# Chunk 5 of each up projection by seven block products instead of eight

## The chip, the cores and the metric

The program runs on one core of one Trainium2 chip. The metric is the device time of one execution in microseconds (us), the median of several runs. TensorE (PE) does the matrix products and loads their stationary operand in a queue of its own (PEld), VectorE (DVE) and ScalarE (ACT) do the elementwise work, GpSimd (POOL) very little, and SyncE (SP) issues the loads of the weights.

## The reference

The reference is a decoder trunk of two layers on 256 tokens of 1024 columns, in float32. Each layer is a half-weighted feed-forward, a token mixer, and a second half-weighted feed-forward; a final RMSNorm follows. So there are four feed-forwards, and the change concerns these alone:

```python
D_MODEL, SEQ, D_FF = 1024, 256, 2816
def swiglu(h, w_up, w_down):
    gate, up = jnp.split(h @ w_up, 2, axis=-1)     # w_up: 1024 x 5632
    return (jax.nn.silu(gate) * up) @ w_down       # w_down: 2816 x 1024
# four times:
x = x + 0.5 * swiglu(rmsnorm(x, norm), w_up, w_down)
```

## The kernel before

Every float32 operand is split in two, `hi` (a rounded copy) and `lo` (what is left), and each product of the reference is three matmuls (`mm3`, lines 302 to 304): hi by hi, hi by lo, lo by hi, added up in PSUM. The stationary operand is a 128 by 128 piece of the transposed activations (`xT_hi`, `xT_lo`), the moving one a piece of the weights.

The weights come in blocks of 128 by 1024 elements (512 KB), in the one order that the list `stream` gives. `feed` (line 180 on) makes a block ready: a load on SP's queue into a buffer `w`, a rounded copy into `hi` on ACT (line 200), and a subtraction into `lo` on DVE (line 201). `block` hands the next block to the matmuls and has fed four further ones by then (`LOOKAHEAD = 4`); there are five `hi` and five `lo` buffers, so the copy for a block waits until PE has finished the block five places ahead of it. The order of the instructions on each engine is laid down when the program is built: an operation whose inputs will be there may be put ahead of one that the code names earlier.

A feed-forward (`ffn`) computes `gate` and `up` in column chunks of 512 (`CW`). 2816 columns make five whole chunks, 0 to 4, and a chunk 5 with 256 columns of gate and 256 of up. Chunk 0 is done plainly. Chunks 1 and 3 are done by seven block products in Winograd's form of Strassen's scheme (`seven_and`, line 445 on): tokens, contraction and (gate, up) are each cut in two halves, and seven products P1 to P7 of half-sized blocks take the place of eight. In return the weights have to be added up in four ways (`form`, line 160 on, DVE adds at line 163; their operands lie in ten buffers `raw`), seven blocks have to be split instead of four for the same work, and the products have to be combined (DVE at line 416, results in buffers `post`). Their blocks alternate in `stream` with those of a plain chunk, 2 or 4, which forms the pair (1, 2) and the pair (3, 4).

Chunk 5 follows the pair (3, 4). It is done plainly: four blocks, each of two rows of 128 by 512 columns (256 of gate, 256 of up, loaded by two transfers of 256 KB), and for each row of 128, each of the two token halves and each of the three parts one matmul of 512 columns: 48 matmuls. Its outputs go through SiLU (ACT, line 420) and a product (DVE, line 425), and `turn` transposes them on PE (line 436) and splits them into `gT_hi` and `gT_lo` (lines 256, 257). `turn` starts two blocks after it was spawned, so the eight transposes of chunk 3 fall into chunk 5. Then the down projection (`y`) runs: two halves of 11 blocks, 12 matmuls of 512 columns each.

Of the kernel before, what the change touches and what calls it, by code (L numbers as in the profile page):

```python
# [15 lines left out]
ALU = mybir.AluOpType  # L16
# [3 lines left out]
P = 128  # L20
D = 1024
S = 256
NT = S // P
KD = D // P
FF = 2816
# [3 lines left out]
CW = 512  # L29
BLK = 1024  # L30
# [15 lines left out]
def trunk(ctx, tc, a, out):  # L46
    nc = tc.nc
# [11 lines left out]
    def pA(name):  # L59
        return psA.tile([P, CW], F32, tag="acc", name=name)  # L60

    def pB(name):
        return psB.tile([P, CW], F32, tag="mx", name=name)
# [7 lines left out]
    def cut(runs):  # L71
        r = []
        for k0, nk, n, cols in runs:
            kb = min(nk, BLK // n)
            for k in range(k0, k0 + nk, kb):
                kk = min(kb, k0 + nk - k)
                at, pieces = 0, []
                for w, c, m in cols:
                    pieces.append((at, m, w[k * P:(k + kk) * P, c:c + m].rearrange("(k p) c -> p k c", p=P)))
                    at += m  # L80
                r.append((kk, n, pieces))
        return r
# [3 lines left out]
    def one(w, k0, nk, c, n=CW):  # L86
        return (k0, nk, n, [(w, c, n)])

    def seven(w, c, mate):

        def cols(c):
            return (c * CW, FF + c * CW)

        def quarter(i, j, p):
            r0 = (4 * i + 2 * p) * P
            return w[r0:r0 + 2 * P, cols(c)[j]:cols(c)[j] + CW].rearrange("(k p) c -> p k c", p=P)

        gate, up = (cut([one(w, 0, 8, x)]) for x in cols(mate))
        st = {}
        r = []  # L100
        for x in SEVEN:
            if x[0] == "P":
                r += [(x, p, st, quarter) for p in range(2)]
            else:
                r.append((gate if x[0] == "G" else up)[int(x[1])])
        return r

    def up_runs(w, first=False):
        r, c = [], 0
        while c < 5:  # L110
            mate = dict(PAIRS).get(c)
            if mate is None:
                g, u = c * CW, FF + c * CW
                r += cut(([one(w, 0, 1, g), one(w, 1, 1, g), one(w, 2, 6, g)] if first and c == 0 else
                          [one(w, 0, 8, g)]) + [one(w, 0, 8, u)])
                c += 1
            else:
                r += seven(w, c, mate)
                c = mate + 1
        return r + cut([(0, 8, CW, [(w, 5 * CW, 256), (w, FF + 5 * CW, 256)])])  # L120

    def down_runs(w):
        return [one(w, 0, KF, 0), one(w, 0, KF, CW)]
# [23 lines left out]
    spool = [None]  # L147
    loaded = [0]

    def load(x, p, st, quarter):  # L150

        def raw(nm):
            if nm not in st:
                st[nm] = spool[0].tile([P, BLK], F32, tag="raw", name="raw", bufs=RAW_BUFS)
            return st[nm]

        for nm, i, j in {"P1": (("a", 0, 0),), "P6": (("b", 0, 1), ("d", 1, 1)), "P2": (("c", 1, 0),)}.get(x, ()):
            nc.sync.dma_start(out=raw(nm + str(p)).rearrange("p (k n) -> p k n", n=CW), in_=quarter(i, j, p))

    def form(x, p, st):  # L160

# [18 lines left out]
    def feed():  # L180
        i = pos[1]
        while loaded[0] < len(stream) and loaded[0] <= i + LEAD:
            if isinstance(stream[loaded[0]][0], str):
                if spool[0] is None:
                    break
                load(*stream[loaded[0]])
            loaded[0] += 1
        pos[1] += 1
        hi = wpool.tile([P, BLK], F32R, tag="hi", name=f"hi{i}", bufs=S_BUFS)
        lo = wpool.tile([P, BLK], F32R, tag="lo", name=f"lo{i}", bufs=S_BUFS)  # L190
        if isinstance(stream[i][0], str):
            k, n = 2, CW
            w = form(*stream[i][:3])
        else:
            k, n, pieces = stream[i]
            w = wpool.tile([P, BLK], F32, tag="w", name=f"w{i}", bufs=W_BUFS)
            wv = w[:, :k * n].rearrange("p (k n) -> p k n", n=n)
            for at, m, src in pieces:
                nc.sync.dma_start(out=wv[:, :, at:at + m], in_=src)
        nc.scalar.copy(out=hi[:, :k * n], in_=w[:, :k * n])  # L200
        nc.vector.tensor_tensor(out=lo[:, :k * n], in0=w[:, :k * n], in1=hi[:, :k * n].bitcast(F32), op=ALU.subtract)  # L201
        ready.append((k, hi[:, :k * n].rearrange("p (k n) -> p k n", n=n),
                      lo[:, :k * n].rearrange("p (k n) -> p k n", n=n)))
# [12 lines left out]
    def spawn(g, steps=1):  # L216
        tasks.append(g)
        speed[g] = steps
        return g
# [81 lines left out]
    def mm3(ps, xh, xl, wh, wl, start, stop, more=False):  # L301
        nc.tensor.matmul(ps, lhsT=xh, rhs=wh, start=start, stop=False, skip_group_check=more)  # L302
        nc.tensor.matmul(ps, lhsT=xh, rhs=wl, start=False, stop=False, skip_group_check=more)  # L303
        nc.tensor.matmul(ps, lhsT=xl, rhs=wh, start=False, stop=stop, skip_group_check=more)  # L304

    def xs_run(pss, hi, lo, k0, nk, kmin=0, kmax=KD - 1, t_major=False):

        k = k0
        while k < k0 + nk:
            kk, wh, wl = block()  # L310
            parts = [(k + i, wh[:, i, :], wl[:, i, :]) for i in range(kk)]
            k += kk
            if t_major and k + 4 > k0 + nk:
                while k < k0 + nk:
                    kk, wh, wl = block()
                    parts += [(k + i, wh[:, i, :], wl[:, i, :]) for i in range(kk)]
                    k += kk
            order = [(p, t) for p in parts for t in range(NT)]
            if t_major and k == k0 + nk:
                order.sort(key=lambda o: o[1])  # L320
            for (ki, whi, wli), t in order:
                mm3(pss[t], hi[:, ki, t * P:(t + 1) * P], lo[:, ki, t * P:(t + 1) * P], whi, wli,
                    ki == kmin, ki == kmax)
            tick()
# [45 lines left out]
    def ffn(n, nxt):  # L370
        with tc.tile_pool(name="gpool", bufs=1) as gpool:
# [30 lines left out]
            def product(x, ps, more=False):  # L402

                hi, lo = forms[x]
                for p in range(2):
                    kk, wh, wl = block()
                    for i in range(kk):
                        mm3(ps, hi[:, 2 * p + i, :], lo[:, 2 * p + i, :], wh[:, i, :], wl[:, i, :],
                            not more and p == 0 and i == 0, p == 1 and i == kk - 1, more)
                    tick()  # L410

            def post(nm):
                return gpool.tile([P, CW], F32, tag="post", name=nm, bufs=4)

            def tt(out, in0, in1, op=ALU.add):
                nc.vector.tensor_tensor(out=out, in0=in0, in1=in1, op=op)

            def silu(src, t, width=CW):
                s = work.tile([P, CW], F32, tag="og", name="s")
                nc.scalar.activation(out=s[:, :width], in_=src, func=AF.Silu, scale=n.rstd[:, t:t + 1])  # L420
                return s

            def times(src, s, t, width=CW):
                g = work.tile([P, CW], F32, tag="on", name="g")
                nc.vector.scalar_tensor_tensor(out=g[:, :width], in0=src, scalar=n.rstd[:, t:t + 1],
                                               in1=s[:, :width], op0=ALU.mult, op1=ALU.mult)
                return g
# [13 lines left out]
            def chunk_out(c, gate, up, width):  # L441
                gs = [times(up[t], silu(gate[t], t, width), t, width) for t in range(NT)]
                next(spawn(turn(c, gs, width)))

            def seven_and(c, mate):
# [28 lines left out]
                tt(q, pc, q, ALU.subtract)  # L474
                next(spawn(turn(c, [times(q, s0, 0), times(r, s1, 1)], CW)))

            spool[0] = gpool
            whole("P1", 0, 0)
            whole("P2", 1, 0)
            whole("P4", 1, 1)  # L480
            c = 0
            while c < 6:
                if c == 0:
                    sm = spawn(sums())
                if c in dict(PAIRS):
                    finish(sm)
                    seven_and(c, dict(PAIRS)[c])
                    c = dict(PAIRS)[c] + 1
                    continue
                gate = [pA("gate") for _ in range(NT)]  # L490
                up = [pB("up") for _ in range(NT)] if c < 5 else None
                xs_run(gate, xT_hi, xT_lo, 0, 8)
                if c < 5:
                    xs_run(up, xT_hi, xT_lo, 0, 8)
                    chunk_out(c, gate, up, CW)
                else:
                    chunk_out(c, [p[:, :256] for p in gate], [p[:, 256:] for p in gate], 256)
                c += 1
            for hf in range(2):
                y = [pA("y") for _ in range(NT)]  # L500
# [769 lines left out]
```

## Time and profile before

| | us |
|---|---|
| median of 3 runs | 1014.79 (1014.54 to 1015.05) |
| the profiled execution's own time | 1013.34 |
| its span, first to last instruction | 1011.6 |
| PE busy | 993.1 |
| DVE busy | 790.3 |
| ACT busy | 574.7 |
| the four stretches of chunk 5, each | 11.77 to 11.81 |

The profiled execution took 1013.34 us, 1.45 us less than the median of the runs. Times in the rows are microseconds from the start of the span. A matmul's duration in the profile runs past the start of the next one, since they are pipelined; the distance between two starts tells what one costs in a row of them. The same holds for DVE: the distance of two starts is what an operation in a row costs.

### The profile page before, as it was taken

What the parts mean: (1) busy time and instruction counts of PE and PEld (TensorE: products, weight loads), DVE (VectorE), ACT (ScalarE), POOL (GpSimd) and SP (SyncE); (2) the same over time, 40 slices, a digit from 0 to 9 for tenths busy, and PEclk for the clock granted to TensorE, in tenths of its full rate; (3) what the DMA queues carried; (4) which work ended last, traced back from release to release, by engine and by line L of the source; (5) the groups of instructions that cost most, each with busy time, mean ns of one, the idle gap of its engine ahead of it and who ended that gap; (6) DMA issues with size and microseconds to landing.
All of it is one profiled execution on the core that took longest, in us unless ns stands there. A gap on an engine that the chain in (4) does not pass through costs nothing.

```text
span 1011.6 us, 13813 instructions
## 1 busy us (share of the span) xinstructions
PE 993.1 (98%) x5124; PEld 821.3 (81%) x5124; DVE 790.3 (78%) x1075; ACT 574.7 (57%) x785; POOL 29.3 (3%) x40
## 2 busy tenths in 40 slices
PE   7999999999999999999999999999999999999996
PEld 6788888888777888888888888888877888888885
DVE  6999855578996699997549899754779879999553
ACT  7576644578543556665446666644556565666441
POOL 0000000101001000000000000000100000000000
PEclk9999999999999999999999999999999999999999
DMA  9655455765403577336567744556753566644651
GB/s 343 231 199 167 148 193 183 217 184 148 126 23 105 167 263 244 113 109 228 188 187 258 257 131 125 189 192 183 229 167 103 167 206 213 228 147 141 213 167 42
DMA packets 98180, 180.11 MB, mean 178 GB/s; under 512 B 6176, under 2 KB 16560, under 8 KB 98112
## 3 DMA queue, kind: packets, MB, share of 16 engines
q1 hardware_dynamic: 96576, 175.69, 54.0%
q0 software_dynamic: 960, 2.91, 0.9%
q8 instruction: 40, 0.66, 0.3%
q10 hardware_dynamic: 576, 0.61, 0.2%
q14 instruction: 28, 0.23, 0.1%
HBM read 178.15 MB, written 1.05 MB: 177 GB/s over the span
## 4 chain that ended last, share of the span: by engine, by line
PE 90%; DVE 5%; ACT 2%; issue 1%; POOL 1%; DMA 0%; SPq 0%; POOLq 0%; ACTq 0%; DVEq 0%
PE y L302 9%; PE y L304 9%; PE y L303 9%; PE gate L302 6%; PE gate L304 6%; PE gate L303 6%; PE p L303 5%; PE p L304 5%; PE p L302 5%; PE up L302 4%; PE up L303 4%; PE up L304 4%; PE ca L302 2%; PE ca L303 2%; PE ca L304 2%; PE gtr L436 2%
## 5 line engine op out<-in xcount | busy, mean ns | idle before, releaser
L201 DVE TENSOR_TENSOR lo<-w,hi 128x1024 fp32r<-128x1024 f32 (+2 forms) x270 | 324.7, 1213 | 162.4 <-ACT hi L200 161.7
L200 ACT CAST hi<-w 128x1024 fp32r<-128x1024 f32 (+2 forms) x270 | 280.2, 1046 | 222.7 <-PE y L304 134.2
L200 ACT CAST hi<-raw 128x1024 fp32r<-128x1024 f32 x112 | 116.7, 1054 | 92.6 <-PE up L304 37.4
L201 DVE TENSOR_TENSOR lo<-raw,hi 128x1024 fp32r<-128x1024 f32 x112 | 135.0, 1218 | 13.4 <-ACT hi L200 11.5
L302 PE MATMUL y<-hi,gT_hi 128*128 128x512 f32 x352 | 137.6, 391 | 0.0
L304 PE MATMUL y<-hi,gT_lo 128*128 128x512 f32 x352 | 137.1, 389 | 0.0
L303 PE MATMUL y<-lo,gT_hi 128*128 128x512 f32 x352 | 137.0, 389 | 0.0
L302 PE MATMUL gate<-hi,xT_hi 128*128 128x512 f32 x256 | 101.0, 399 | 2.3 <-ACT xT_hi L259 2.1
L304 PE MATMUL gate<-hi,xT_lo 128*128 128x512 f32 x256 | 100.5, 393 | 0.0
L303 PE MATMUL gate<-lo,xT_hi 128*128 128x512 f32 x256 | 100.3, 392 | 0.0
L163 DVE TENSOR_TENSOR raw<-raw 128x1024 f32<-128x1024 f32 x64 | 77.5, 1215 | 0.6 <-DMA raw<-l_ffn_w_up 0.4
L304 PEld LDWEIGHTS y<-hi,gT_lo 128*128 128x128 f32 x352 | 66.0, 188 | 13.9
L303 PEld LDWEIGHTS y<-lo,gT_hi 128*128 128x128 f32 x352 | 66.1, 188 | 13.5
L302 PEld LDWEIGHTS y<-hi,gT_hi 128*128 128x128 f32 x352 | 66.1, 188 | 13.5
L302 PE MATMUL up<-hi,xT_hi 128*128 128x512 f32 x192 | 74.7, 389 | 0.0
L303 PE MATMUL up<-lo,xT_hi 128*128 128x512 f32 x192 | 74.7, 389 | 0.0
L304 PE MATMUL up<-hi,xT_lo 128*128 128x512 f32 x192 | 74.7, 389 | 0.0
L302 PEld LDWEIGHTS gate<-hi,xT_hi 128*128 128x128 f32 x256 | 48.4, 190 | 12.6 <-ACT xT_hi L259 2.5
L304 PEld LDWEIGHTS gate<-hi,xT_lo 128*128 128x128 f32 x256 | 48.3, 189 | 10.2
L303 PEld LDWEIGHTS gate<-lo,xT_hi 128*128 128x128 f32 x256 | 48.6, 190 | 9.6
L303 PE MATMUL p<-lo,fhP 128*128 128x512 f32 x128 | 50.0, 391 | 0.0
L304 PE MATMUL p<-hi,flP 128*128 128x512 f32 x128 | 49.8, 389 | 0.0
(310 smaller groups left out, 1666.3 us busy)
## 6 DMA issues: line engine op xcount, KB each, us to landing
w<-l_ffn_w_up SPq DMA_DIRECT2D x95, 512.0 KB, 4.0
w<-l_ffn_w_down SPq DMA_DIRECT2D x88, 512.0 KB, 3.5
raw<-l_ffn_w_up SPq DMA_DIRECT2D x64, 512.0 KB, 5.1
w<-l_w_in SPq DMA_DIRECT2D x50, 512.0 KB, 3.7
w<-l_ffn_w_up SPq DMA_DIRECT2D x34, 256.0 KB, 3.9
w<-l_w_out SPq DMA_DIRECT2D x16, 512.0 KB, 3.5
x_sb<-x SPq DMA_DIRECT2D x4, 256.0 KB, 4.2
w<-l_w_in SPq DMA_DIRECT2D x2, 396.0 KB, 4.3
```

Of the source, the lines that this page charges most:

```text
L163: nc.vector.tensor_tensor(out=out, in0=in0, in1=in1, op=ALU.add)
L200: nc.scalar.copy(out=hi[:, :k * n], in_=w[:, :k * n])
L201: nc.vector.tensor_tensor(out=lo[:, :k * n], in0=w[:, :k * n], in1=hi[:, :k * n].bitcast(F32), op=ALU.subtract)
L302: nc.tensor.matmul(ps, lhsT=xh, rhs=wh, start=start, stop=False, skip_group_check=more)
L303: nc.tensor.matmul(ps, lhsT=xh, rhs=wl, start=False, stop=False, skip_group_check=more)
L304: nc.tensor.matmul(ps, lhsT=xl, rhs=wh, start=False, stop=stop, skip_group_check=more)
L436: nc.tensor.transpose(ps[:, j * P:(j + 1) * P], gs[t][:, j * P:(j + 1) * P], ident)
```

## The change

Chunk 5 of each of the four feed-forwards is done by seven block products as well, with 256 columns to a block in place of 512, and by itself, with no plain chunk alternating. Its seven blocks P1, P6, P7, P5, P2, P4, P3 each hold four rows of 128 by 256 columns, so that each product is 4 by 3 matmuls of 256 columns: 84 in all. The weights are loaded as four blocks of 512 KB (a, b, d, c) into `raw` buffers in place of eight transfers of 256 KB into `w`. `form` adds t = a + b and u = t + d for P6, b + d for P7, u + c for P4; P5 uses t. `seven_last` is the new function that combines the products, and `product` and `seven` are made general in the number of columns.

```diff
--- before.py
+++ after.py
@@ -86,24 +86,29 @@
     def one(w, k0, nk, c, n=CW):
         return (k0, nk, n, [(w, c, n)])
 
-    def seven(w, c, mate):
-
+    def seven(w, cols, n, order, **between):
+
+        kb = BLK // n
+
+        def quarter(i, j, p):
+            r0 = (4 * i + kb * p) * P
+            return w[r0:r0 + kb * P, cols[j]:cols[j] + n].rearrange("(k p) c -> p k c", p=P)
+
+        st = {}
+        r = []
+        for x in order:
+            if x[0] == "P":
+                r += [(x, p, st, quarter, n) for p in range(4 // kb)]
+            else:
+                r.append(between[x[0]][int(x[1])])
+        return r
+
+    def seven_up(w, c, mate):
         def cols(c):
             return (c * CW, FF + c * CW)
 
-        def quarter(i, j, p):
-            r0 = (4 * i + 2 * p) * P
-            return w[r0:r0 + 2 * P, cols(c)[j]:cols(c)[j] + CW].rearrange("(k p) c -> p k c", p=P)
-
         gate, up = (cut([one(w, 0, 8, x)]) for x in cols(mate))
-        st = {}
-        r = []
-        for x in SEVEN:
-            if x[0] == "P":
-                r += [(x, p, st, quarter) for p in range(2)]
-            else:
-                r.append((gate if x[0] == "G" else up)[int(x[1])])
-        return r
+        return seven(w, cols(c), CW, SEVEN, G=gate, U=up)
 
     def up_runs(w, first=False):
         r, c = [], 0
@@ -115,9 +120,9 @@
                           [one(w, 0, 8, g)]) + [one(w, 0, 8, u)])
                 c += 1
             else:
-                r += seven(w, c, mate)
+                r += seven_up(w, c, mate)
                 c = mate + 1
-        return r + cut([(0, 8, CW, [(w, 5 * CW, 256), (w, FF + 5 * CW, 256)])])
+        return r + seven(w, (5 * CW, FF + 5 * CW), S, ("P1", "P6", "P7", "P5", "P2", "P4", "P3"))
 
     def down_runs(w):
         return [one(w, 0, KF, 0), one(w, 0, KF, CW)]
@@ -147,7 +152,7 @@
     spool = [None]
     loaded = [0]
 
-    def load(x, p, st, quarter):
+    def load(x, p, st, quarter, n):
 
         def raw(nm):
             if nm not in st:
@@ -155,7 +160,7 @@
             return st[nm]
 
         for nm, i, j in {"P1": (("a", 0, 0),), "P6": (("b", 0, 1), ("d", 1, 1)), "P2": (("c", 1, 0),)}.get(x, ()):
-            nc.sync.dma_start(out=raw(nm + str(p)).rearrange("p (k n) -> p k n", n=CW), in_=quarter(i, j, p))
+            nc.sync.dma_start(out=raw(nm + str(p)).rearrange("p (k n) -> p k n", n=n), in_=quarter(i, j, p))
 
     def form(x, p, st):
 
@@ -189,7 +194,8 @@
         hi = wpool.tile([P, BLK], F32R, tag="hi", name=f"hi{i}", bufs=S_BUFS)
         lo = wpool.tile([P, BLK], F32R, tag="lo", name=f"lo{i}", bufs=S_BUFS)
         if isinstance(stream[i][0], str):
-            k, n = 2, CW
+            n = stream[i][4]
+            k = BLK // n
             w = form(*stream[i][:3])
         else:
             k, n, pieces = stream[i]
@@ -402,11 +408,12 @@
             def product(x, ps, more=False):
 
                 hi, lo = forms[x]
-                for p in range(2):
+                k = 0
+                while k < 4:
                     kk, wh, wl = block()
                     for i in range(kk):
-                        mm3(ps, hi[:, 2 * p + i, :], lo[:, 2 * p + i, :], wh[:, i, :], wl[:, i, :],
-                            not more and p == 0 and i == 0, p == 1 and i == kk - 1, more)
+                        mm3(ps, hi[:, k, :], lo[:, k, :], wh[:, i, :], wl[:, i, :], not more and k == 0, k == 3, more)
+                        k += 1
                     tick()
 
             def post(nm):
@@ -474,6 +481,29 @@
                 tt(q, pc, q, ALU.subtract)
                 next(spawn(turn(c, [times(q, s0, 0), times(r, s1, 1)], CW)))
 
+            def seven_last(c):
+
+                pa, pb, pc, pd = (v[:, :S] for v in (pA("p1"), pB("p6"), pA("p5"), pA("p7")))
+                product("P1", pa)
+                q = post("q")[:, :S]
+                nc.scalar.copy(out=q, in_=pa)
+                product("P6", pb)
+                tt(q, q, pb)
+                product("P7", pd)
+                r = post("r")[:, :S]
+                tt(r, q, pd)
+                product("P5", pc)
+                tt(r, pc, r, ALU.subtract)
+                product("P2", pa, True)
+                s0 = silu(pa, 0, S)
+                product("P4", pd, True)
+                g1 = post("g1")[:, :S]
+                tt(g1, q, pd)
+                s1 = silu(g1, 1, S)
+                product("P3", pc, True)
+                tt(q, pc, q, ALU.subtract)
+                next(spawn(turn(c, [times(q, s0, 0, S), times(r, s1, 1, S)], S)))
+
             spool[0] = gpool
             whole("P1", 0, 0)
             whole("P2", 1, 0)
@@ -487,14 +517,14 @@
                     seven_and(c, dict(PAIRS)[c])
                     c = dict(PAIRS)[c] + 1
                     continue
+                if c == 5:
+                    seven_last(c)
+                    break
                 gate = [pA("gate") for _ in range(NT)]
-                up = [pB("up") for _ in range(NT)] if c < 5 else None
+                up = [pB("up") for _ in range(NT)]
                 xs_run(gate, xT_hi, xT_lo, 0, 8)
-                if c < 5:
-                    xs_run(up, xT_hi, xT_lo, 0, 8)
-                    chunk_out(c, gate, up, CW)
-                else:
-                    chunk_out(c, [p[:, :256] for p in gate], [p[:, 256:] for p in gate], 256)
+                xs_run(up, xT_hi, xT_lo, 0, 8)
+                chunk_out(c, gate, up, CW)
                 c += 1
             for hf in range(2):
                 y = [pA("y") for _ in range(NT)]
```

## Rows read from the trace of the kernel before

**Rows 1.** The page: busy time of the engines, and the chain that ended last.
```profile
PE 993.1 (98%) x5124; PEld 821.3 (81%) x5124; DVE 790.3 (78%) x1075; ACT 574.7 (57%) x785; POOL 29.3 (3%) x40
...
PE 90%; DVE 5%; ACT 2%; issue 1%; POOL 1%; DMA 0%; SPq 0%; POOLq 0%; ACTq 0%; DVEq 0%
```

**Rows 2.** Windows, second feed-forward: PE, PEld, DVE, ACT, POOL busy, clock, DMA share, GB/s.
```profile
415.30:458.00 42.70, 42.70 (x199) 35.47 (x198) 40.62 (x42) 27.30 (x32) 0.00 (x0) 1.00 0.43 131
458.00:469.80 11.80, 11.80 (x58) 9.83 (x57) 9.55 (x11) 6.03 (x8) 0.00 (x0) 1.00 0.85 285
469.80:532.00 62.20, 62.20 (x282) 51.56 (x281) 32.61 (x34) 27.69 (x34) 0.00 (x0) 1.00 0.59 187
```

**Rows 3.** Windows: chunk 5 of the first feed-forward.
```profile
118.77:130.54 11.77, 11.77 (x57) 9.84 (x56) 9.54 (x11) 6.07 (x8) 0.00 (x0) 1.00 0.84 284
```

**Rows 4.** Timeline, PE, second feed-forward: chunk 5 starts, transposes, the down projection starts.
```profile
457.98 0.39 PE L302 MATMUL gate<-hi,xT_hi 128*128 128x512 f32 x1
...
463.42 1.04 PE L436 MATMUL gtr<-ident,g 128*128 128x128 f32 x8
...
469.78 0.39 PE L302 MATMUL y<-hi,gT_hi 128*128 128x512 f32 x1
```

**Rows 5.** Timeline, PE: first and last of 36 matmuls of 256 columns in a row.
```profile
234.34 0.28 PE L302 MATMUL rk<-hi,xT_hi 128*128 128x256 f32 x1
...
238.53 0.28 PE L304 MATMUL rk<-hi,xT_lo 128*128 128x256 f32 x1
```

**Rows 6.** Timeline, DVE, around the start of chunk 5 in the second feed-forward.
```profile
454.48 2.36 DVE L201 TENSOR_TENSOR lo<-w,hi 128x1024 fp32r<-128x1024 f32 x2
456.75 0.68 DVE L416 TENSOR_TENSOR g<-q,p 128x512 f32<-128x512 f32 x1
457.35 2.35 DVE L201 TENSOR_TENSOR lo<-w,hi 128x1024 fp32r<-128x1024 f32 x2
...
461.36 0.74 DVE L425 SCALAR_TENSOR_TENSOR g<-q,rstd,s 128x512 f32<-128x512 f32 x1
462.02 0.74 DVE L425 SCALAR_TENSOR_TENSOR g<-r,rstd,s 128x512 f32<-128x512 f32 x1
462.68 1.22 DVE L201 TENSOR_TENSOR lo<-w,hi 128x1024 fp32r<-128x1024 f32 x1
```

**Rows 7.** Windows, DVE alone, ahead of chunk 5 (busy, clock, DMA share, GB/s).
```profile
443.00:454.50 11.50, 9.53 (x12) 1.00 0.13 44
```

**Rows 8.** Timeline, DVE, the same place between pair (1, 2) and pair (3, 4).
```profile
403.76 1.22 DVE L163 TENSOR_TENSOR raw<-raw 128x1024 f32<-128x1024 f32 x1
...
407.36 1.21 DVE L163 TENSOR_TENSOR raw<-raw 128x1024 f32<-128x1024 f32 x1
...
411.96 2.35 DVE L201 TENSOR_TENSOR lo<-raw,hi 128x1024 fp32r<-128x1024 f32 x2
```

**Rows 9.** Timeline, PE: P2 of the pair (1, 2) and of the pair (3, 4) starts.
```profile
406.28 0.39 PE L302 MATMUL p<-hi,xT_hi 128*128 128x512 f32 x1
...
448.92 0.39 PE L302 MATMUL p<-hi,xT_hi 128*128 128x512 f32 x1
```

**Rows 10.** Groups by line and shape: copies on ACT, adds of `form`, split of 256 columns.
```profile
L200 ACT CAST hi<-w 128x1024 fp32r<-128x1024 f32 x265 | 276.7, 1052 | 217.3 <-PE y L304 134.2 <-PE gate L304 22.0 <-PE ca L304 15.8
...
L163 DVE TENSOR_TENSOR raw<-raw 128x1024 f32<-128x1024 f32 x64 | 77.5, 1215 | 0.6 <-DMA raw<-l_ffn_w_up 0.4
...
L257 DVE TENSOR_TENSOR gT_lo<-gtr,gT_hi 128x256 fp32r<-128x256 f32 x8 | 3.0, 416 | 0.0
```

**Rows 11.** Timeline, all engines: a late `lo` of P6 in the pair (3, 4).
```profile
424.76 1.22 DVE L201 TENSOR_TENSOR lo<-raw,hi 128x1024 fp32r<-128x1024 f32 x1
...
426.03 0.62 PE L302 MATMUL gate<-hi,xT_hi 128*128 128x512 f32 x2
...
426.48 0.39 PE L303 MATMUL p<-lo,fhP 128*128 128x512 f32 x1
```

**Rows 12.** The page: issues of loads, from issue to landing.
```profile
raw<-l_ffn_w_up SPq DMA_DIRECT2D x64, 512.0 KB, 5.1
```

## The prediction

> **What bounds the kernel now.** I read the page first: PE is busy for 98% of the span, and the chain that ended last runs through PE for 90% of it [rows 1]. A busy PE need not be a PE that moves, since matmuls overlap in the records, so I went on to the distances between starts. Through the pair (3, 4), chunk 5 and the down projection of the second feed-forward, matmuls start one behind another without a hole: 24 matmuls of 512 columns between 457.98 and 463.42, 0.2267 us each, and 24 more plus eight transposes up to 469.78, which leaves 0.92 us for the transposes [rows 4]. So PE sets the pace, and each microsecond that it waits is lost for good, because the down projection behind it has PE busy throughout its 62.2 us [rows 2].
>
> The windows show who is next. In the pair (3, 4) DVE is busy 40.6 of 42.7 us, in chunk 5 9.6 of 11.8, in the down projection half the time [rows 2]. The pair lives at the limit of DVE; chunk 5 is the place where DVE regains its lead (its four blocks need only 4 times 1.14 us). The change puts DVE work into that place. Chunk 5 takes 11.77 us in the first feed-forward and 11.80 in the second [rows 3, 4]; I take the four as alike.
>
> **What PE gains.** Removed: 48 matmuls of 512 columns, 48 x 0.2267 = 10.88 us. Added: 84 of 256 columns. The kernel has such matmuls with the same operands, 36 in a row from 234.34 to 238.53, 35 steps of 0.1197 us [rows 5]; 84 of them take 10.06 us. The saving is 0.82 us to a feed-forward, 3.3 in all, if every block is there when PE wants it. No more is to be had from PE: the transposes stay.
>
> **What DVE and ACT have to do for it.** In chunk 5 of one feed-forward:
> - Splits: seven blocks instead of four, so three more copies on ACT (1.05 us each [rows 10]; ACT is busy only 6.0 of 11.8 us there [rows 2], so they fit) and three more subtractions on DVE.
> - Four adds of 1024 columns (t, u, b + d, u + c) on DVE. They last 1215 ns [rows 10], but in a row a DVE operation of this size starts 1.14 us after the last (two subtractions from 454.48, the next thing at 456.75 [rows 6]); 1.14 is what I use.
> - Combining: five DVE operations of 128 by 256 in addition to the two products with SiLU that were there, and one copy on ACT. One of 512 columns lasts 0.68 and costs 0.60 (456.75 to 457.35 [rows 6]); one of 256 lasts 0.416 [rows 10], so about 0.34.
>
> Sum on DVE: 7 x 1.14 + 5 x 0.34 = 9.7 us more in a stage that PE would pass in 10.06 + 0.92 = 10.98.
>
> **Can DVE be early enough?** This is a sum along DVE's queue, in the second feed-forward. The nearest thing in the trace is the passage from the pair (1, 2) to the pair (3, 4), where the same P1 and P6 come next. There the adds t and u run far ahead, at 403.76 and 407.36, and the subtraction for P1 starts at 411.96 [rows 8], 5.68 us after P2 of the old pair started on PE at 406.28; P2 of the pair (3, 4) starts at 448.92 [rows 9]. So I expect t and u in the places that correspond, and P1's subtraction at 448.92 + 5.68 = 454.60. Before, it starts at 454.48 [rows 6]: the two adds (2.28 us) go into idle time, of which DVE has 11.50 - 9.53 = 1.97 us there [rows 7]. Nothing more can be put earlier: what idle time there was is used up.
>
> From 454.60 on, the work that stands ahead of the last block, P3, is: the subtractions of the seven blocks, 7.98; the adds for P7 and P4, 2.28; the pair's own g and q, 0.60 each; its two products with SiLU, 0.66 each (461.36, 462.02, 462.68 [rows 6]); two splits of chunk 3's transposes, 1.20; and q and r of chunk 5, 0.68. Together 14.66 us: P3 is ready at 469.26. In between each block is ready about when PE wants it (P6 at 456.9, P7 at 460.9 against 460.9, P2 at 464.0 against 463.8).
>
> PE, unhindered, starts chunk 5 at 457.98 [rows 4] and P3 six products (6 x 1.436) and the transposes (0.92) later, at 467.52. The first matmul of P3 needs only hi, the second needs lo: it is due at 467.64 and can start at 469.3. **PE waits some 1.65 us, twice what the seven products save.** The last eleven matmuls end at 470.6, against 469.78 now: 0.84 us later. The first block of the down projection follows on DVE 1.14 to 1.48 us behind P3's, at 470.4 to 470.7, so it adds little; after that, a block of the down projection gives PE 2.7 us for DVE's 1.14 and the lead returns.
>
> **What lies beside it.** The loads: 4 of 512 KB in place of 8 of 256 KB, the same bytes in SP's queue; `raw` loads take 5.1 us to land [rows 12]. The engines of the DMA are at 13% there [rows 7]. Of the ten `raw` buffers the pair still holds four by then (d and u, twice each; a, b and t are done with P1, P7 and P5, c soon after), which leaves the six that chunk 5 needs: a, b, d, t, u, c. The down projection's loads no longer share the `w` buffers with chunk 5, so they come earlier; they are hidden either way. If a load came late by its whole 5.1 us it would add that to the wait, and I see no reason for it. PSUM: the bank for P1 is free early, once the pair's `up` has been multiplied; those for P5 and P7 when g and q of the pair are done on DVE, in the sum above at 457.5 and 461.5, while PE wants the second of them at 460.9 to 462.4. That can cost from 0 to 0.6 us; I take 0. [...]
>
> **The size of the wait, from both sides.** Below: the order of the work on PE is not that of the text. In the pair (3, 4), where the subtraction for P6 started only at 424.76, two matmuls that need hi alone (of another block) were put in at 426.03, and P6 went on at 426.48 with no hole [rows 11]. In chunk 5 two matmuls of the down projection can fill 0.45 us of the wait in the same way, and two splits of the transposes (1.20) could stand behind P3's subtraction instead of ahead of it. With both, the wait is gone, and the stage saves up to 0.82. Above: for P7 and for P4 the subtraction must wait for an add and then for ACT's copy, 1.05 us [rows 10]. I assumed that DVE does other work meanwhile; if it stands idle both times, P3 is 2.1 us later.
>
> [...]
>
> **Sum.** 0.84 a stage, and a little given back by matmuls put ahead: 0.8 x 4 = 3.3 us more. The profiled execution took 1013.34 us (its span is 1011.6, with 1.7 around it); with 3.3 it would take 1016.6. The median of the runs is 1014.79, 1.45 above the profiled one, so I forecast **1018.1**.
>
> **The rivals.** About 0.2% (2.0 us) is what this measurement can tell from no change.
> - *Forecast: DVE makes PE wait for the last products by one to two times the saving.* 2 to 6 us slower, 1017 to 1021. Chance 0.48. For it: DVE at 95% in the pair [rows 2], and no idle time left ahead of chunk 5.
> - *The wait eats the saving and no more.* Matmuls that need hi alone fill a part, or a split of the transposes moves back; the wait is 0.3 to 1.3 us a stage, and the run within 2 us of before. Chance 0.23.
> - *The other side: the lead covers it.* If the splits of the transposes (1.20) and two matmuls of the down projection (0.45) both move, they make 1.65 us, just the wait, and the whole saving stands: 1014.79 - 3.3 = 1011.5. It decides from a wait under 0.3 us a stage. For it: PE takes the pair's DVE load, 95%, without a hole. Against: it needs everything that can be moved. Chance 0.13.
> - *Idle DVE behind the adds.* The chain add, copy on ACT, subtraction is exposed for P7 and P4: 2.1 us more a stage, 3.3 + 8.4 = 11.7, so 1026. Against: the pair has eight such adds, and DVE idles for only 42.70 - 40.62 = 2.08 us in all of it [rows 2], so other work is found. Chance 0.16, with what lies between.
>
> So: faster 0.13, same 0.23, slower 0.64. The likeliest case reaches from 1017 to 1021; the range that leaves out no more than 2 in 10 runs from the other side's 1011.8 to 1024, short of the full price of the exposed chain.
>
> **What would show it.** In chunk 5, 84 matmuls of 256 columns with a distance of 0.12 us wherever they run; t and u ahead of the pair's last subtractions; P1's subtraction near 454.6 in the second feed-forward; DVE without idle time from there until P3's; a hole on PE, or matmuls of `y` moved ahead, before the second matmul of P3 (or spread over P2, P4 and P3); `y` starting 0.4 to 1 us later than now, four times over; the down projection as long as before. I am wrong if the order of DVE puts the transposes' splits behind P3, if a load or a bank of PSUM is what PE waits for, or if matmuls of 256 columns start further apart than 0.12 here, where they change their stationary operand as often as before but DVE is busier.

## The result: 1.2% slower, four times the forecast

The changed kernel takes 1027.26 us (median of 4 runs, 1024.47 to 1028.23) against 1014.66 for the kernel before on the same occasions: a ratio of 1.0122, 95% interval 1.0109 to 1.0134. Forecast was 1018.1, with a range to 1024.0. The direction was right, the size was not, and the time lies outside the range.

The page of the changed kernel: busy time of the engines, and the chain that ended last (for [rows 1]).

```profile
PE 999.7 (97%) x5268; PEld 831.2 (81%) x5268; DVE 826.3 (81%) x1123; ACT 586.6 (57%) x801; POOL 29.3 (3%) x40
...
PE 82%; DVE 12%; issue 3%; ACT 2%; DMA 1%; POOL 0%; SPq 0%; POOLq 0%; ACTq 0%; DVEq 0%
```

DVE is busy for 36 us more, 9.0 a feed-forward, where the prediction summed 9.7. The chain of waits now runs through DVE for 12% of the span instead of 5%. That share says where to look and not how much is lost: the run below with banks of their own is 10 us faster and has the same 12%.

Chunk 5 of the second feed-forward, PE's timeline (for [rows 4]): its first matmul, the third product (P7), the last matmul of the fifth (P2), what follows, and the 40th matmul of the down projection.

```profile
462.03 0.28 PE L308 MATMUL p<-hi,xT_hi 128*128 128x256 f32 x1
...
464.90 0.71 PE L308 MATMUL p<-hi,fhP 128*128 128x256 f32 x2
465.93 0.39 PE L309 MATMUL p<-lo,fhP 128*128 128x256 f32 x1 [0.32 <-DVE lo L207]
...
470.88 0.28 PE L310 MATMUL p<-hi,xT_lo 128*128 128x256 f32 x1
471.00 0.39 PE L308 MATMUL y<-hi,gT_hi 128*128 128x512 f32 x1
471.73 0.49 PE L308 MATMUL y<-hi,gT_hi 128*128 128x512 f32 x1 [0.34 <-ACT s L427]
473.66 0.39 PE L308 MATMUL p<-hi,xT_hi 128*128 128x256 f32 x1 [1.44 <-DVE r L423]
473.88 0.28 PE L309 MATMUL p<-lo,xT_hi 128*128 128x256 f32 x1
...
475.14 0.41 PE L310 MATMUL p<-hi,xT_lo 128*128 128x256 f32 x1
475.35 0.63 PE L309 MATMUL y<-lo,gT_hi 128*128 128x512 f32 x1
475.78 0.41 PE L308 MATMUL p<-hi,fhP 128*128 128x256 f32 x1
475.99 0.41 PE L309 MATMUL p<-lo,fhP 128*128 128x256 f32 x1
...
487.05 0.39 PE L308 MATMUL y<-hi,gT_hi 128*128 128x512 f32 x1
```

The first five products have one hole, at P7: two matmuls that need hi alone start at 464.90, and the next at 465.93, when the subtraction for P7 is done on DVE. Two such matmuls in a row take 0.24 us, so this hole is 0.79 us. P4 is due at 471.00 and starts at 473.66. Two matmuls of `y` that need only hi were put into the wait, as the prediction expected, but the wait is for `r` on DVE at line 423, a combining add, and not for a subtraction. From 475 on the distance of two starts is 0.21 us and no longer 0.12: the clock has fallen. P3 (from 475.78) does not wait; the matmul of `y` ahead of it takes 0.43 us at the lower clock. Windows of PE show it (busy us, granted clock, DMA share, GB/s):

```profile
471.00:475.00 4.00, 2.23 (x15) 1.00 0.00 0
475.00:478.40 3.40, 3.40 (x17) 0.50 0.63 169
478.40:485.00 6.60, 6.60 (x33) 1.00 0.95 324
```

For 3.4 us the granted clock is 0.50 instead of 1.00, after 4 us in which PE was busy for 2.2. The same happens in the third and the fourth feed-forward (0.50 from 659.30 and from 956.26, for 3.41 us each); in the first the same hole, 130.06 to 131.99, is followed by no fall (1.00 from 130 to 140).

What a stage costs can be read as the distance from the first matmul of chunk 5 to the 40th of the down projection, since all the holes lie before that one (in the second feed-forward 462.03 to 487.05 here, and 457.98 to 479.12 before). For the four feed-forwards:

| | 1 | 2 | 3 | 4 | falls of the clock |
|---|---|---|---|---|---|
| before | 21.09 | 21.14 | 21.14 | 21.09 | 0 |
| after | 23.52 | 25.02 | 25.00 | 24.98 | 3 |

So a stage loses 2.4 us without a fall of the clock, and a fall costs 1.5 more. The sum is 2.43 + 3.88 + 3.86 + 3.89 = 14.1 us. Between these stretches the two traces agree within 0.1 us (318.12 and 318.15 from the first to the second chunk 5, for one). The span is 14.8 us longer; the rest is the start, 1.6 us (chunk 5 of the first feed-forward starts at 120.36, before at 118.77; until 14.2 instead of 11.4 us the first matmuls of 512 columns start 0.43 us apart, from then on 0.23; in the ten traces of this case this step comes anywhere between 11.1 and 14.4, and in the two kernels without seven products in chunk 5 at 11.4 and 13.8, so this is not the change), and the end behind the last matmul of `y`, which is 0.9 us shorter than in the trace before.

DVE in the same stretch (for [rows 6 and 8]):

```profile
450.34 1.22 DVE L168 TENSOR_TENSOR raw<-raw 128x1024 f32<-128x1024 f32 x1
...
455.46 1.22 DVE L168 TENSOR_TENSOR raw<-raw 128x1024 f32<-128x1024 f32 x1
...
458.93 2.35 DVE L207 TENSOR_TENSOR lo<-raw,hi 128x1024 fp32r<-128x1024 f32 x2
461.20 0.68 DVE L423 TENSOR_TENSOR g<-q,p 128x512 f32<-128x512 f32 x1
461.79 1.22 DVE L168 TENSOR_TENSOR raw<-raw 128x1024 f32<-128x1024 f32 x1
462.93 0.68 DVE L423 TENSOR_TENSOR q<-p,q 128x512 f32<-128x512 f32 x1
463.53 1.21 DVE L168 TENSOR_TENSOR raw<-raw 128x1024 f32<-128x1024 f32 x1
464.66 2.35 DVE L207 TENSOR_TENSOR lo<-raw,hi 128x1024 fp32r<-128x1024 f32 x2
...
470.53 1.28 DVE L263 TENSOR_TENSOR gT_lo<-gtr,gT_hi 128x512 fp32r<-128x512 f32 x2
471.73 0.41 DVE L423 TENSOR_TENSOR q<-q,p 128x256 f32<-128x256 f32 x1
472.06 1.21 DVE L207 TENSOR_TENSOR lo<-raw,hi 128x1024 fp32r<-128x1024 f32 x1
473.19 0.41 DVE L423 TENSOR_TENSOR r<-q,p 128x256 f32<-128x256 f32 x1
473.52 1.22 DVE L207 TENSOR_TENSOR lo<-w,hi 128x1024 fp32r<-128x1024 f32 x1
474.66 0.41 DVE L423 TENSOR_TENSOR r<-p,r 128x256 f32<-128x256 f32 x1
```

The second feed-forward starts chunk 5 4.05 us later than before (462.03 against 457.98). With that, t was forecast for 450.5 and came at 450.34, P1's subtraction for 458.65 and came at 458.93, and P3's was to end at 473.31 and ended at 472.06 + 1.21 = 473.27. So the sum along DVE's queue gave the right end. In between it did not: P7's subtraction, forecast to be done at 460.9, that is 464.95 here, is the first of the two from 464.66 and done at about 465.8, for the pair's two combining adds (461.20, 462.93), the add for P7 and the one for P4 (463.53) all stand ahead of it. This makes the hole at P7. By the trace that hole adds nothing to the end, because what PE waits for later comes in its turn on DVE, which is not idle from 458.93 to 478.

What the sum left out stands in the last lines: r = q + P7, a small add, comes behind P3's subtraction, and r = P5 - r behind one for the down projection. P4 adds to the very bank of PSUM in which P7 lies (`product("P4", pd, True)`), so it may not start before DVE has read P7 for r (which ends at 473.19 + 0.41 = 473.60; P4 starts at 473.66); P3 adds to the bank of P5 in the same way.

### The profile page after: what moved, and what is told of

Same layout as the page of the kernel before. It is cut to its first block, busy times and chain, and to the rows that moved or that the text cites. A ratio compares the mean times of both kernels' runs of the same rounds, so it can differ in the third digit from the quotient of the medians.

```text
span 1026.4 us, 14157 instructions
## 1 busy us (share of the span) xinstructions
PE 999.7 (97%) x5268; PEld 831.2 (81%) x5268; DVE 826.3 (81%) x1123; ACT 586.6 (57%) x801; POOL 29.3 (3%) x40
## 4 chain that ended last, share of the span: by engine, by line
PE 82%; DVE 12%; issue 3%; ACT 2%; DMA 1%; POOL 0%; SPq 0%; POOLq 0%; ACTq 0%; DVEq 0%
PE y L309 9%; PE y L310 9%; PE y L308 9%; PE p L308 4%; PE p L309 4%; PE p L310 4%; DVE lo L207 4%; PE gate L310 4%; PE gate L309 4%; PE gate L308 4%; PE up L308 4%; PE up L309 4%; PE up L310 4%; PE ca L308 2%; PE ca L309 2%
## 5 line engine op out<-in xcount | busy, mean ns | idle before, releaser
L206 ACT CAST hi<-raw 128x1024 fp32r<-128x1024 f32 x140 | 144.6, 1054 | 94.6 <-DVE raw L168 33.9
L207 DVE TENSOR_TENSOR lo<-raw,hi 128x1024 fp32r<-128x1024 f32 x140 | 168.2, 1218 | 8.4 <-ACT hi L206 6.8
L308 PE MATMUL gate<-hi,xT_hi 128*128 128x512 f32 x192 | 76.0, 401 | 2.7 <-ACT xT_hi L265 2.4
L310 PE MATMUL gate<-hi,xT_lo 128*128 128x512 f32 x192 | 75.9, 396 | 0.0
L309 PE MATMUL gate<-lo,xT_hi 128*128 128x512 f32 x192 | 75.8, 395 | 0.0
L309 PE MATMUL p<-lo,fhP 128*128 128x512 f32 (+1 forms) x192 | 70.1, 366 | 1.3 <-DVE lo L207 1.3
L308 PE MATMUL p<-hi,fhP 128*128 128x512 f32 (+1 forms) x192 | 69.7, 363 | 0.1
L310 PE MATMUL p<-hi,flP 128*128 128x512 f32 (+1 forms) x192 | 69.3, 362 | 0.0
L308 PE MATMUL p<-hi,xT_hi 128*128 128x512 f32 (+1 forms) x144 | 52.4, 364 | 5.8 <-DVE r L423 5.8
L310 PE MATMUL p<-hi,xT_lo 128*128 128x512 f32 (+1 forms) x144 | 51.6, 359 | 0.0
```

## The experiments

Three theories. **A, the bank**: P4 and P3 wait until DVE has read the bank that they add to, and these reads stand too far back in DVE's queue. **B, the load**: as predicted, the amount of DVE's work sets the end, in whatever order. **C, the clock**: the falls after the hole make a large part of it. Ratios are to the kernel before, with 95% intervals.

**Three blocks ahead.** Inside chunk 5, blocks are fed three ahead instead of four, which puts the small adds ahead of the subtractions for P4 and P3.

```diff
-        while pos[1] < len(stream) and pos[1] <= pos[0] + LOOKAHEAD:
+        while pos[1] < len(stream) and pos[1] <= pos[0] + ahead[0]:
...
             def seven_last(c):
...
+                ahead[0] = 3
                 product("P1", pa)
...
+                ahead[0] = LOOKAHEAD
                 product("P4", pd, True)
```

> Inside chunk 5 blocks are fed three ahead instead of four, so that the subtractions for P4 and P3 are named behind q + P6 and r = q + P7 and no longer ahead of them. Theory A (the bank): P4 adds to the bank that holds P7, so it waits until DVE has read that bank for r = q + P7, and this small add stands behind the subtraction for P3 in DVE's queue. By A the hole before P4 (1.93 us from start to start) falls under 1 us, a stage takes 12.6 to 13 us instead of 14.2 to 15.6, the clock does not fall, and the run takes 1017 to 1020. Theory B (the load, as in the prediction): the sum of DVE's work sets the end whatever its order; P3's subtraction moves back by what is put ahead of it, and the run stays at 1024 to 1028. [...]

Measured: 1018.47 us, ratio 1.0035 (1.0022 to 1.0048). The work is the same, its order alone is not, and some 9 us are gone: theory A holds, B as an account of the whole falls. A stage takes 22.41 to 22.48 us to the 40th matmul of `y`, which is 13.1 us without these 40 (9.33 us in the kernel before), a little over the 12.6 to 13 that A gave; the clock does not fall (its mean is 0.998 to 0.999 in all five runs). The hole is shorter, and still one for `r`:

```profile
470.39 0.49 PE L309 MATMUL y<-hi,gT_hi 128*128 128x512 f32 x1 [0.34 <-ACT s L428]
471.23 0.39 PE L309 MATMUL p<-hi,xT_hi 128*128 128x256 f32 x1 [0.34 <-DVE r L424]
```

**Banks of their own for P4 and P3.** The same order of blocks as in the change; the two products no longer touch the banks that DVE reads, at the price of two more small adds on DVE.

```diff
-                product("P4", pd, True)
                 g1 = post("g1")[:, :S]
                 tt(g1, q, pd)
-                s1 = silu(g1, 1, S)
-                product("P3", pc, True)
                 tt(q, pc, q, ALU.subtract)
+                pe, pf = pA("p4")[:, :S], pB("p3")[:, :S]
+                product("P4", pe)
+                tt(g1, g1, pe)
+                s1 = silu(g1, 1, S)
+                product("P3", pf)
+                tt(q, q, pf)
```

> P4 and P3 get PSUM banks of their own instead of adding to those of P7 and P5, and DVE adds them in two more operations of 256 columns (0.34 us each). Theory A: P4 starts once its subtraction is done, about 0.3 us behind P2, P3 at about its own subtraction; a stage takes 12.6 to 13 us, the clock does not fall, 1017 to 1020. Theory B: P3's subtraction ends where it did or 0.3 later; the run stays at 1024 to 1028 or is slightly slower.

Measured: 1016.94 us, ratio 1.0021 (1.0012 to 1.0031), at the lower edge of A's forecast. A stage takes 22.05 to 22.09 us, 0.97 more than before; the clock does not fall (its mean is 0.998 to 0.999 in all ten runs). P7 waits as it did, 0.79 us; P4 no longer waits. P3 does, 0.55 us, and now for its subtraction, as the prediction had it (PE, then DVE, second feed-forward):

```profile
470.43 0.28 PE L308 MATMUL p<-hi,fhP 128*128 128x256 f32 x1
470.55 0.39 PE L308 MATMUL y<-hi,gT_hi 128*128 128x512 f32 x1
471.33 0.39 PE L309 MATMUL p<-lo,fhP 128*128 128x256 f32 x1 [0.38 <-DVE lo L207]
```

```profile
470.06 1.21 DVE L207 TENSOR_TENSOR lo<-raw,hi 128x1024 fp32r<-128x1024 f32 x1
471.19 0.41 DVE L423 TENSOR_TENSOR r<-q,p 128x256 f32<-128x256 f32 x1
```

`r` still comes after P3's subtraction, but no matmul waits for it any longer.

**Both together.** On top of the banks of their own, blocks are fed three ahead.

```diff
...
+                ahead[0] = 3
                 product("P1", pa)
...
+                ahead[0] = LOOKAHEAD
                 product("P4", pe)
```

> Own banks for P4 and P3, and blocks fed three ahead inside chunk 5. If what is left of the loss with own banks alone (22.07 us from the first matmul of chunk 5 to the 40th of the down projection, 21.1 before) is P3's subtraction standing at the end of DVE's queue, as in the prediction, the order changes nothing more: 1016 to 1018. If it is a small add that still stands in the wrong place, the two together gain what each gained: 1013 to 1015.

Measured: 1018.27 us, ratio 1.0038 (1.0024 to 1.0052), a little above the first of the two forecasts and far from the second; a stage takes 22.34 to 22.37. No gain over own banks, rather a loss of 0.28 a stage: with the bank out of the way, feeding three ahead only makes blocks later. P4's subtraction now stands behind q + P6 and the splits of the transposes, and PE waits at P4's second matmul (470.63), which was due at 469.53; one matmul of P3 and one of `y` that need hi alone fill a part of the wait (PE, then DVE, second feed-forward):

```profile
469.53 0.28 PE L309 MATMUL p<-hi,fhP 128*128 128x256 f32 x1
470.14 0.50 PE L309 MATMUL y<-hi,gT_hi 128*128 128x512 f32 x1 [0.33 <-ACT s L428]
470.63 0.39 PE L310 MATMUL p<-lo,xT_hi 128*128 128x256 f32 x1
```

```profile
469.36 1.22 DVE L208 TENSOR_TENSOR lo<-raw,hi 128x1024 fp32r<-128x1024 f32 x1
```

So what is left of the loss with own banks is not a small add in the wrong place.

**Without the four adds.** Own banks, and t, u, b + d and u + c are left out, so that DVE has 4.6 us less.

```diff
...
+        if n == S:
+            return g[{"P1": "a", "P6": "a", "P7": "b", "P5": "a", "P2": "c", "P4": "c", "P3": "d"}[x]]
         if x == "P6":
...
```

> As with own banks, but the four adds on the weights of chunk 5 are left out (P6 and P5 take block a, P7 b, P4 c as they were loaded), so the output is not the reference's. DVE has 4.6 us less a stage and nothing runs on POOL in its place. If the amount of DVE's work is the rest of the loss (theory B for the rest), PE waits no more, the stretch to the 40th matmul of the down projection takes 20.3 to 20.5 us (21.1 less 0.82) and the run 1011 to 1013. If the loss lies with PE, ACT's copies or the loads, it stays at 1016 to 1017.

Measured: 1010.97 us, ratio 0.9968 (0.9956 to 0.9980). A stage takes 20.48 to 20.54 us, 0.6 less than before, of the 0.82 that PE can save. In the second feed-forward chunk 5 starts at 458.18 and `y` at 469.34: 11.16 us, where 84 matmuls and the transposes were forecast at 10.98.

```profile
458.18 0.28 PE L310 MATMUL p<-hi,xT_hi 128*128 128x256 f32 x1
...
469.34 0.40 PE L310 MATMUL y<-hi,gT_hi 128*128 128x512 f32 x1
```

The waits at P7 and at P3 are both gone. The run takes away the adds' time on DVE and at once the chain of add, copy and subtraction that the prediction's last rival is about. That it is the time that counts is read from the trace with own banks: DVE has no idle time there from 7.5 us before chunk 5 to 20 us after its start, so no chain can have left it idle. So the rest of the loss is the load on DVE: theory B holds for what A leaves.

**The adds on POOL.** The same 4.6 us taken from DVE, but done on the idle engine.

```diff
-            nc.vector.tensor_tensor(out=out, in0=in0, in1=in1, op=ALU.add)
+            (nc.gpsimd if n == S else nc.vector).tensor_tensor(out=out, in0=in0, in1=in1, op=ALU.add)
...
```

> The four adds on the weights of chunk 5 (t, u, b + d, u + c) go from DVE to POOL; nothing else changes. DVE has 4.6 us less a stage. Theories A and B alike: every wait in the stage goes, since 4.6 us is more than the hole; a stage takes 11.0 to 11.5 us and the run 1011 to 1014, if an add on POOL takes under 3 us and does not slow DVE. If POOL needs over 4 us for an add, or DVE's operations get longer beside it, the blocks P6 and P7 come late and the run is at 1017 or above.

Measured: 1035.79 us, ratio 1.0210 (1.0195 to 1.0225), the slowest of all. An add on POOL takes 2.98 us on average, and a subtraction that DVE starts while one runs takes up to 3.42 us instead of 1.22 (POOL, then DVE, second feed-forward):

```profile
450.33 9.07 POOL L168 TENSOR_TENSOR raw<-raw 128x1024 f32<-128x1024 f32 x3 [87.48 <-DVE lo L207]
```

```profile
450.39 3.42 DVE L207 TENSOR_TENSOR lo<-raw,hi 128x1024 fp32r<-128x1024 f32 x1
453.73 0.68 DVE L423 TENSOR_TENSOR r<-p,r 128x512 f32<-128x512 f32 x1
454.33 6.16 DVE L207 TENSOR_TENSOR lo<-raw,hi 128x1024 fp32r<-128x1024 f32 x2
```

Three subtractions took 9.6 us instead of 3.4 beside three adds: 6.2 us lost to spare 3.4. The combining operation `r`, with an operand in PSUM, took 0.68 us there as without the adds on POOL. By the trace the four stages lose 12.9 us together, and some 8 more are lost between them, where the adds for P6 and P7 fall into the pair ahead of chunk 5; two falls of the clock, one in the first chunk 5 and one in the last pair, are in this (the mean clock is 0.995 in the traced run).

**The hole filled.** The changed kernel with eight matmuls between P2 and P4 whose result nobody reads.

```diff
                 s0 = silu(pa, 0, S)
+                fill = pT("fill")
+                for _ in range(8):
+                    nc.tensor.matmul(fill, lhsT=xT_hi[:, 0, 0:P], rhs=gT_hi[:, 0:2, :].rearrange("p k n -> p (k n)"),
+                                     start=True, stop=True)
                 product("P4", pd, True)
```

> Eight matmuls of 512 columns whose result nobody reads are put between P2 and P4 (1.8 us of work for PE, about as long as the hole). [...] Theories A and B say nothing of the clock: by them P4 starts when it did, and the stage without a fall (14.2 us) is unchanged. If the falls come all the same, the time is 1025 to 1028.

Measured: 1022.94 us, ratio 1.0081 (1.0064 to 1.0098), inside the 1021 to 1023 of theory C, by which the 4 to 5 us of the three falls come back when PE has work in the hole. The clock does not fall (its mean is 0.998 to 0.999 in all four runs), and all four stages take 23.48 to 23.51 us, what the stage without a fall took in the changed kernel. So theory C holds for its part: the three falls cost 1.5 us each, 4.5 of the 12.6, and they do not come with the hole filled. The rest of the loss, 2.4 us a stage, is untouched by it.

```profile
469.66 0.39 PE L308 MATMUL y<-hi,gT_hi 128*128 128x512 f32 x1
469.93 2.14 PE L501 MATMUL fill<-gT_hi,xT_hi 128*128 128x512 f32 x8
471.90 0.39 PE L308 MATMUL y<-hi,gT_hi 128*128 128x512 f32 x1
472.32 0.38 PE L308 MATMUL p<-hi,xT_hi 128*128 128x256 f32 x1
```

**The seven products spread over the down projection.** All the adds stay on DVE, P4 and P3 add to the banks of P7 and P5 as in the change, but from P6 on a block of the down projection stands between each two products, and P7's bank comes from the pool of P6's.

```diff
+    SPREAD = ("P1", "P6", "D0", "P7", "D1", "P5", "D2", "P2", "D3", "P4", "D4", "P3", "D5", "D6", "D7", "D8", "D9", "DA")
...
-                pa, pb, pc, pd = (v[:, :S] for v in (pA("p1"), pB("p6"), pA("p5"), pA("p7")))
+                pa, pb, pc, pd = (v[:, :S] for v in (pA("p1"), pB("p6"), pA("p5"), pB("p7")))
                 product("P6", pb)
                 tt(q, q, pb)
+                down(1)
                 product("P7", pd)
                 r = post("r")[:, :S]
                 tt(r, q, pd)
+                down(1)
...
```

> The seven products of chunk 5 with all their adds, on DVE, but alternating with the first blocks of the down projection (P1, P6, D0, P7, D1, P5, D2, P2, D3, P4, D4, P3, D5 and on); P7 goes to a bank of the pool of P6. DVE's extra 9.7 us then lies beside 10 us plus 14 us of PE. If DVE's work and the two banks are all that made the change slower, PE waits for nothing and the saving of 0.82 us a stage stands: 1011 to 1013, below before. If the alternation brings waits of its own (banks, the raw buffers, order), 1015 or above.

Measured: 1010.80 us, ratio 0.9964 (0.9952 to 0.9977): faster than both kernels, and a little faster than forecast. Windows of the stretch from chunk 5 on in the second feed-forward (busy PE, PEld, DVE, ACT, POOL, clock, DMA share, GB/s):

```profile
457.17:488.00 30.83, 30.83 (x182) 27.22 (x181) 26.19 (x30) 18.60 (x22) 0.00 (x0) 1.00 0.52 169
```

DVE is busy 26.2 of 30.8 us, where in the changed kernel's chunk 5 it was busy all the time; no start on PE in chunk 5 or the down projection comes more than 0.1 us late. From the last matmul of the pair (3, 4) to the last of the down projection it is 72.33, 72.38, 72.37 and 71.46 us, against 72.99, 73.06, 73.06 and 72.09 before: 0.63 to 0.69 less, most of the 0.82. The four together are 2.66 of the 3.6 us between the medians; in the traces the rest lies mostly behind the last matmul of `y`, where the trace of the kernel before is 0.9 us longer than all nine others.

**Its control: the plain chunk 5, alternating.** The kernel before, with the four plain blocks between the first of the down projection.

```diff
...
+                    for i in range(4):
+                        xs_run(gate, xT_hi, xT_lo, 2 * i, 2)
+                        if i == 3:
+                            chunk_out(5, [p[:, :256] for p in gate], [p[:, 256:] for p in gate], 256)
+                        xs_run(y, gT_hi, gT_lo, 2 * i, 2, kmax=KF - 1)
+                    xs_run(y, gT_hi, gT_lo, 8, KF - 8, kmax=KF - 1, t_major=nxt is None)
```

> Control for the alternation: the kernel before, with the four plain blocks of chunk 5 alternating with the first four of the down projection. PE has the same matmuls and waited for nothing before, so no change: 1014 to 1015.5. If alternation by itself gains or loses, it shows here, and is to be taken from the run with seven products.

Measured: 1013.90 us, ratio 0.9994 (0.9985 to 1.0003): no change. The gain of the run with seven products, 3.1 us against this control, is theirs and not that of the alternation.

## Why the prediction was wrong, step by step

- **What bounds, and who is next**: right. PE sets the pace, and DVE has no room in the pair.
- **What PE gains**: right. Matmuls of 256 columns run at 0.12 us, and without waits a stage is 0.6 to 0.7 us shorter, where 0.82 was forecast.
- **The sum along DVE's queue**: right in its end, not on the way. Set against the later start of chunk 5, t, P1's and P6's subtractions came within 0.3 us of the forecast, but u came 1.4 us late, P7's subtraction 0.9 late and P2's 1.4 late; "each block is ready about when PE wants it" failed at P7, with the hole of 0.79 us. P3's came within 0.04, and that is partly luck: the sum began 0.28 us late, and one item of it, 0.34 us, was in the wrong place. "q and r of chunk 5, 0.68" were put ahead of P3's subtraction; only q stood there, and r came after it.
- **The banks: the step that failed.** The prediction asked when the banks for P5 and P7 come free for chunk 5, took 0 for it, and did not ask when they may be added to again, though "a bank of PSUM is what PE waits for" stands among its own signs of being wrong. P4 and P3 go into the banks of P7 and P5 once DVE has read these. With banks of their own, and two small adds more on DVE, the loss is 0.97 us a stage, against the 0.84 of the sum (with the wait split between P7 and P3, and not all at P3); with the shared banks 2.4. Three blocks ahead, which moves only the order, brings it to 1.3. The wait is P4's for r, at 2.66 us (471.00 to 473.66), 0.45 of it filled with `y`, and not P3's at 1.65.
- **The clock: a second step that failed.** The sum counts a wait of PE at its own length, and no row of the kernel before shows what a hole of 2 us costs. Three of four holes were followed by 3.4 us at a granted clock of 0.50, 1.5 us each, which the filled hole gave back.
- **The rivals.** The 1026 of the exposed chain of adds came nearest in time, by luck: it rests on DVE standing idle behind the adds, and DVE has no idle time from 458.93 until 478 in the second feed-forward.
- **"The other side"**: as priced. It did not come about in the changed kernel; with the waits gone, in the run without the adds and in the one spread over the down projection, the time is 1010.8 to 1011.0, where 1011.5 was forecast.
- **Loads**: hidden, as taken; no matmul of chunk 5 waits for one.

Added up, from runs: 4 x 0.97 us for DVE's load (own banks), 4 x 1.45 more for the bank, up to 3 x 1.5 for the clock, 14.2 us with all three falls, beside 14.1 in the traces of the stages and 12.6 between the medians. How many falls the runs without a trace had is not shown. The mean clock is 0.994 in the three slower runs, the traced one with its three falls among them, and 0.997 in the one at 1024.47. An estimate: 3.413 us at half the clock take 0.0017 off the mean of a run of 1026 us, so 0.997 is about two falls fewer than 0.994 (the runs of the kernel before show 0.997 to 0.999, so this is rough). That run is 2.6 to 3.8 us faster than the others, about two falls of 1.5 us.

## What to carry to other kernels

In a program like this one, a product that is added into a bank whose earlier content another engine has still to read waits for that reader, wherever the reader stands in its engine's queue (here P4 for `r`, 2.66 us): list the readers of a bank for each time that it is written again, not only for the first. Work that is saved on the engine that sets the pace at the price of the engine next to it belongs beside a stretch where the latter has time: the same seven products lose 12 us as one block and gain 3.6 when they alternate with the down projection. And a hole on PE may be paid twice, as the one of 1.93 us was here in three of four places: once as it passes and once by 3.4 us at half the clock, which cost 1.5 us more.

## What was not expected of the hardware

- The fall of the clock is not a matter of the hole alone: the same hole (1.93 us between two starts, with 0.73 before it) was followed by 3.413 us at a granted clock of 0.50 in three stages of the changed kernel and by none in the first.
- POOL and DVE slowed each other down in the run with the adds on POOL. A float32 add of 128 by 1024 on POOL took 2.4 us where no subtraction was under way on DVE at its start, and 3.3 to 3.5 us where one was. A subtraction of that size that started while such an add ran took 2.1 to 3.4 us instead of 1.22; one that had started before kept its 1.22.
